# Norm means by rounded matmuls, and four smaller matmul jobs of a decoder trunk recast

## The chip, the cores and the metric

The kernel runs on one core of a Trainium2 chip. The time is device microseconds of that core, the median of several runs. Its engines are named as the profile names them: PE (matmuls; PEld is its weight load), DVE, ACT, POOL and SP. All of a launch's work is in one program; each engine works through its own list of instructions in order and waits on semaphores for the others. Matmul results stand in PSUM, in banks of 128 x 512 numbers.

## The reference

One sequence of 512 tokens with 1024 features passes four steps, each behind a root-mean-square norm: an attention layer (MLA), a squared-ReLU MLP, a gated linear attention (GLA) and a second MLP. A last norm ends it. All is float32.

```python
def rms_norm(x, gain):
    y = x * rsqrt(mean(x * x, axis=-1) + EPS)
    return y * gain

for i in range(2):
    xn = rms_norm(x, norm_mix[i])
    x = x + (mla_mixer(xn, ...) if i == 0 else gla_mixer(xn, ...))
    x = x + square(relu(rms_norm(x, norm_mlp[i]) @ w_up[i])) @ w_down[i]
return rms_norm(x, final_norm)

# MLA: a low-rank latent c_kv is normed too, and gives keys and values
kv = rms_norm(c_kv, kv_norm) @ w_ukv
# GLA, within a chunk of 64 tokens; b is the running sum of the log gates, per feature
attn[t, s] = sum_d q[t, d] * k[s, d] * exp(b[t, d] - b[s, d])     # for s <= t
```

On the diagonal of attn the decay is 1, so attn[t, t] is the sum over d of q k alone.

## The kernel before

Activations lie with features on the 128 partitions and the 512 tokens along the free axis, so x is eight tiles of 128 x 512 (xT). A product is made of three rounded ones: each float32 operand is split into a rounded high part (the type fp32r, an ACT copy) and the low rest (a DVE subtraction), and PE adds high x high, high x low and low x high. That is `mm3` (L120 to L122); the split is `split` (L112 on ACT, L115 on DVE). Where an operand isn't split, PE multiplies in full float32.

`Norm` keeps a running total `acc` of the squares of the eight tiles (ACT squares, DVE adds, L238). `mean` (L255) multiplies `acc` by a constant matrix of 1/1024 in full float32, one product of 512 columns, which sums over the partitions and lays the mean on all of them; `rsqrt` then makes 1/rms. For GLA's input the mean is taken in `finish`, which `a_pair` calls ahead of step k = 5 of the first pair of projections. For each MLP, which runs as a seven-product block scheme on combined operands (`QuadNorm`; T1 to T4 and the x tiles), the place is written out by hand: block steps are popped from two lists, then `combine` of the last row, the mean, some idle products into a scratch bank (`spare`, L1181) and the split of the last combined rows.

In MLA the 1/rms of three norms come as rows (`rows`, 96 x 512: three groups of 32 like rows; L221 ends it). The one for the values is needed on all partitions: a full-precision product of a one-row operand spreads it (L532, bank `wide`), ACT copies it to SBUF (L534), and DVE scales the latent with it (L537). Around it stand the v products and their evacuations (L504 to L508), the rotary tables (L392, with a table load of ACT ahead and one behind), the rotary q products and the key's transposes (L137 of `KS`).

In GLA, 1/rms per token is turned onto the partitions by four one-column products (L1334) and a copy (L1336). Two heads are worked at a time between the projection products. For each head `T` holds gate factors; `grow(m)` scales q and k by them, `same` makes the diagonal of the attention matrix by four 128 x 128 full products (L1454), of which a masked copy (L1455) takes the diagonal, and `small(m)` makes the blocks next to it, for m = 1 up, each by two 128-column full products (L1467) with an ACT copy (L1447) as operand.

The order of the instructions on each engine is set by a scheduler from the order of the code, except where the code says `kept` or `issue_after`. PSUM banks go round by tag: `bank("c")` takes the next bank of that ring.

## Time and profile before

| | before |
|---|---|
| median of 3 runs | 1048.47 us (1047.91 to 1049.2) |
| profiled execution | 1048.56 us, span 1046.5 us, granted clock 0.998 |
| PE / PEld busy | 1037.0 us / 957.7 us |
| DVE / ACT / POOL busy | 858.0 / 645.2 / 92.6 us |

The span runs from the first to the last instruction of the profiled execution, and its time is 2.1 us longer. MLA lasts to about 154 us, its output projection to 188, the first MLP to about 507, GLA with its output projection to 723, the second MLP to about 993. In the chain of waits "x2" counts records, not products: a full-precision product leaves two. The chain dates a matmul from the end of the one before it, about 0.16 us later than the timeline, which dates it from its own start.

### The profile page before, as it was taken

The numbers are of one execution on the slowest core, as the hardware profiler recorded it, in microseconds if no ns is written. First come the engines' busy times: TensorE is split into PE (matmuls) and PEld (weight loads), VectorE is DVE, ScalarE is ACT, GpSimd is POOL, SyncE is SP. The second block draws the span as 40 slices with busy tenths as digits, with TensorE's granted clock in tenths as the row PEclk, the third lists the DMA queues.
The fourth block names the chain that finished last, engine by engine and source line by source line (L and its number), as shares of the span: only waits on it lengthen the run. The fifth ranks groups of instructions, "written<-read, shape, count | busy, mean of one in ns | idle before, by whom it ended". The sixth has DMA issues, their size and how long they took to land.

```text
span 1046.5 us, 17929 instructions
## 1 busy us (share of the span) xinstructions
PE 1037.0 (99%) x7252; PEld 957.7 (92%) x7252; DVE 858.0 (82%) x1236; ACT 645.2 (62%) x969; POOL 92.6 (9%) x118
## 2 busy tenths in 40 slices
PE   8999999999999999999999999999999999999997
PEld 7788888999999999998788888888999999999986
DVE  6789879899899789976576656678999899799855
ACT  5678755666667777654344645656666667776834
POOL 6400000100000000270000000001000000000000
PEclk9999999999999999999999999999999999999999
DMA  6412016866654664351122221239565655653402
GB/s 200 114 50 63 20 41 200 183 181 162 182 136 128 181 147 119 98 187 55 51 81 81 81 79 56 68 101 230 174 145 155 182 134 152 180 133 90 146 37 81
DMA packets 114946, 127.81 MB, mean 122 GB/s; under 512 B 8640, under 2 KB 86736, under 8 KB 114864
## 3 DMA queue, kind: packets, MB, share of 16 engines
q1 hardware_dynamic: 98832, 108.15, 32.6%
q0 software_dynamic: 13792, 16.80, 10.5%
q10 hardware_dynamic: 2240, 1.73, 0.5%
q8 instruction: 57, 0.93, 0.4%
q14 instruction: 25, 0.20, 0.1%
HBM read 124.56 MB, written 2.10 MB: 121 GB/s over the span
## 4 chain that ended last, share of the span: by engine, by line
PE 98%; DMA 1%; DVE 0%; issue 0%; ACT 0%; SPq 0%; DVEq 0%
PE ps L844 51%; PE ps L120 13%; PE ps L122 13%; PE ps L121 13%; PE ps L137 2%; PE ps L1467 1%; DMA wraw_ckv<-in_mla_w_in_dram 1%; PE ps L1502 1%; PE ps L696 0%; PE ps L695 0%; PE ps L692 0%; PE ps L693 0%; PE ps L694 0%; PE ps L1454 0%; PE ps L255 0%; PE ps L1356 0%
## 5 line engine op out<-in xcount | busy, mean ns | idle before, releaser
L112 ACT ACTIVATE wh<-raw 128x1024 fp32r<-128x1024 f32 x208 | 219.4, 1058 | 133.0 <-PE ps L844 74.9
L115 DVE TENSOR_TENSOR wl<-raw,wh 128x1024 fp32r<-128x1024 f32 x208 | 252.0, 1221 | 18.6 <-ACT wh L112 18.2
L844 PE MATMUL ps<-h,wh 128*128 128x256 f32 x1344 | 166.6, 276 | 0.0
L844 PEld LDWEIGHTS ps<-h,wh 128*128 128x128 f32 x1344 | 159.2, 188 | 0.0
L120 PE MATMUL ps<-set,wh 128*128 128x512 f32 x232 | 91.5, 395 | 1.0 <-ACT set L245 1.0
L121 PE MATMUL ps<-set,wh 128*128 128x512 f32 x232 | 91.0, 392 | 0.7 <-DVE set L246 0.6
L122 PE MATMUL ps<-set,wl 128*128 128x512 f32 x232 | 90.6, 391 | 0.0
L844 PE MATMUL ps<-h,wl 128*128 128x256 f32 x672 | 90.1, 276 | 0.0
L897 POOL DMA_DIRECT2D raw<-in_mlp_w_up_dram x20 | 25.8, 1291 | 688.0 <-DVE raw L950 307.3
L844 PEld LDWEIGHTS ps<-h,wl 128*128 128x128 f32 x672 | 82.7, 188 | 0.0
L112 ACT ACTIVATE wh<-wraw 128x1024 fp32r<-128x1024 f32 x41 | 43.1, 1057 | 53.2 <-PE ps L121 25.8
L909 ACT ACTIVATE q<-q 128x512 f32<-128x512 f32 x64 | 40.3, 631 | 51.5 <-DVE q L908 51.5
L115 DVE TENSOR_TENSOR h<-q,h 128x1024 fp32r<-128x1024 f32 x44 | 53.6, 1219 | 9.0 <-ACT h L112 9.0
L120 PE MATMUL ps<-wh,set 128*128 128x512 f32 x144 | 59.5, 413 | 0.0
L121 PE MATMUL ps<-wl,set 128*128 128x512 f32 x144 | 56.3, 391 | 0.0
L122 PE MATMUL ps<-wh,set 128*128 128x512 f32 x144 | 56.2, 391 | 0.0
L115 DVE TENSOR_TENSOR wl<-wraw,wh 128x1024 fp32r<-128x1024 f32 x41 | 50.4, 1229 | 6.8 <-ACT wh L112 6.6
L120 PEld LDWEIGHTS ps<-set,wh 128*128 128x128 f32 x232 | 43.5, 188 | 10.7 <-ACT set L245 1.7
L121 PEld LDWEIGHTS ps<-set,wh 128*128 128x128 f32 x232 | 43.6, 188 | 10.4 <-DVE set L246 1.4
L122 PEld LDWEIGHTS ps<-set,wl 128*128 128x128 f32 x232 | 43.6, 188 | 9.0
L112 ACT ACTIVATE h<-q 128x1024 fp32r<-128x1024 f32 x44 | 46.0, 1048 | 0.9 <-DVE q L1057 0.6
L121 PE MATMUL ps<-hl,wh 128*128 128x512 f32 x96 | 37.4, 389 | 0.0
(522 smaller groups left out, 2780.6 us busy)
## 6 DMA issues: line engine op xcount, KB each, us to landing
raw<-in_mlp_w_down_dram SPq DMA_DIRECT2D x38, 1024.0 KB, 5.2
raw<-in_mlp_w_up_dram SPq DMA_DIRECT2D x70, 512.0 KB, 5.2
wraw<-in_gla_w_in_dram SPq DMA_DIRECT2D x11, 1024.0 KB, 5.3
raw<-in_mlp_w_up_dram POOLq DMA_DIRECT2D x20, 512.0 KB, 7.3
raw<-in_mlp_w_down_dram POOLq DMA_DIRECT2D x6, 1024.0 KB, 9.3
wraw<-in_mla_w_o_dram SPq DMA_DIRECT2D x8, 512.0 KB, 4.9
wraw<-in_gla_w_o_dram SPq DMA_DIRECT2D x8, 512.0 KB, 4.9
wraw_qn<-in_mla_w_uq_dram SPq DMA_DIRECT2D x6, 256.0 KB, 3.4
```

The source lines that it names most:

```text
L112: raised.append(order(ACT.activation(hi, src, AF.Copy)))
L115: return lo_eng.tensor_tensor(lo, src, f(hi), ALU.subtract)
L120: PE.matmul(psum, wh, xh, start=start, stop=False, **kw)
L121: PE.matmul(psum, wh, xl, start=False, stop=False, **kw)
L122: PE.matmul(psum, wl, xh, start=False, stop=stop, **kw)
L137: PE.transpose(psum, src, ident[: src.shape[0], : src.shape[0]])
L844: return PE.matmul(p[:, m * TH : (m + 1) * TH], w[i][:, k - k0, m * P : (m + 1) * P], x[k][j], start=start, stop=stop, skip_group_check=True,)
L897: POOL.dma_start(t, rows(half, trail), accum_op=ALU.add)
L909: ACT.activation(qs, qs, AF.Square)
L1467: PE.matmul(p[:, :, r], side[m][:, sl], joined(o, e), start=True, stop=True)
L1502: PE.matmul(out_, kj, mv, start=True, stop=True)
```

## The change

Six places change.

1. The constant of the means is rounded, and `parted` splits `acc` into a high part (ACT, in the buffer of 1/rms) and a low part (DVE). `mean` is two rounded products. In the MLPs the split stands between the two block steps ahead of the last combined rows, with the second step's, and the last rows', evacuations ordered behind it; the spare products are three instead of four. For GLA's input the mean moves from step 5 to step 6.
2. In MLA four copies within SBUF, issued by ACT, lay the 32 like rows onto all 128 partitions, in place of the product and its copy.
3. In GLA, 1/rms per token comes from a product with the identity and a sum along the row, both on DVE.
4. The diagonal comes from q k on DVE, split, and summed over the partitions by four rounded products of 256 columns with a matrix of ones.
5. The blocks of m = 1 likewise, by two rounded products; their ACT copy goes.
6. One MLP operand buffer always stands at the same offset. The last norm's two products read the constant as full float32.

```diff
@@ -179,12 +179,8 @@
     DVE.memset(causal, 0.0)
     POOL.affine_select(causal, causal, [[-1, P]], ALU.is_ge, NEG, base=0, channel_multiplier=1)
 
-    def inv_tile(n, pool):
-        t = pool.tile([P, P], F32, name=f"inv{n}")
-        DVE.memset(t, 1.0 / n)
-        return t
-
-    inv_d = inv_tile(D, const)
+    inv_d = const.tile([P, P], F32R, name="inv_d")
+    DVE.tensor_scalar(inv_d, ones128, 1.0 / D, None, ALU.mult)
 
 
 
@@ -250,12 +246,18 @@
             self.scaled(j, src)
             self.square(src)
 
-        def mean(self):
+        def parted(self, order=lambda i: i):
+            self.parts = sb.tile([P, S], F32R, tag="rstd", bufs=1, name=uname("acc_hi")), tmp((P, S), F32R)
+            return order(split(self.acc, *self.parts, order=order))
+
+        def mean(self, order=lambda i: i):
             self.ms = bank("c")
-            return PE.matmul(self.ms, self.inv, self.acc, start=True, stop=True)
+            for n, part in enumerate(self.parts):
+                order(PE.matmul(self.ms, self.inv, part, start=n == 0, stop=n == 1))
 
         def finish(self):
             if self.ms is None:
+                self.parted()
                 self.mean()
             m = self.ms
             r = sb.tile([P, S], F32, tag="rstd", bufs=1, name=uname("rstd"))
@@ -406,7 +408,7 @@
 
     def a_pair(psums, w, nrm):
         for k in range(ND):
-            if k == 5:
+            if k == 6:
                 nrm.finish()
             for j in range(2):
                 mm3(psums[j], cut(w[j], slice(None), k), nrm.out[k], k == 0, k == ND - 1)
@@ -489,6 +491,9 @@
         PE.matmul(means, mean_q, q_sq[0], start=False, stop=True)
         rows = sb.tile([3 * RB, S], F32, tag="rstd", bufs=1, name=uname("rstd"))
         rsqrt(rows, means, S, row_eps)
+        r_kv = f(slot("B"))
+        for i in range(P // RB):
+            ACT.dma_start(r_kv[i * RB : (i + 1) * RB], rows[:RB])
 
 
         raw = pool_of("stage").tile([P, 2, MH, VD], F32, tag="wraw", bufs=2, name="wraw_v")
@@ -528,10 +533,6 @@
                 else:
                     evac_v(t, hf, p)
             if t == 1:
-                wide = bank("c")
-                PE.matmul(wide, ones128[0:1], rows[0:1], start=True, stop=True)
-                r_kv = sb.tile([P, S], F32, tag="rstd", bufs=1, name=uname("rstd"))
-                ACT.activation(r_kv, wide, AF.Copy)
                 for j in range(2):
                     y = tmp()
                     DVE.scalar_tensor_tensor(y, pkv[j], gcol("kvn", 2 * layer + j), r_kv, ALU.mult, ALU.mult)
@@ -859,7 +860,7 @@
             for k, m in steps:
                 one(1, 0, k, m, False, end and k == 3)
 
-        Q, wide, turn, fills = {}, {}, [0, None], []
+        Q, wide, turn, fills = {}, {}, [0], []
 
         def up_block(b):
             fh, s = b % 2, b // 2
@@ -1018,9 +1019,7 @@
                 turn[0] ^= 1
                 if turn[0]:
                     h = dp.tile([P, 8 * TH + 40], F32R, tag="h1", name=uname("h"))
-                    c = 0 if turn[1] != s else 40
-                    h = h[:, c : c + 8 * TH].rearrange("p (i k t) -> p i k t", i=2, k=4)
-                    turn[1] = s
+                    h = h[:, 40:].rearrange("p (i k t) -> p i k t", i=2, k=4)
                 else:
                     h = dp.tile([P, 2, 4, TH], F32R, tag="h0", name=uname("h"))
                 split(t, h[:, 0], h[:, 1])
@@ -1188,14 +1187,18 @@
             wide[b] = halves(wide_raw())
         for b, t in enumerate(halves(wide_raw())):
             fills[b](t)
-        for b in range(2):
-            blocks[b].pop(0)()
+        blocks[0].pop(0)()
+        low = nrm.parted(kept)
+        high = raised[-1]
+        with tc.issue_after(high.ins):
+            blocks[1].pop(0)()
         t = nrm.combine(KH - 1, dp.tile([P, 4, TH], F32, tag="q", bufs=6, name=uname("q")))
-        kept(nrm.mean())
-        spare(mp.tile([P, 4 * TH], F32, tag="d", bufs=2, name=uname("ps")), 4)
+        nrm.mean(kept)
+        spare(mp.tile([P, 4 * TH], F32, tag="d", bufs=2, name=uname("ps")), 3)
         made[1]["21"] = piece(made[1]["a12"], KH, 256)
         kept(cut_at[-1])
-        kept(nrm.combined(KH - 1, t))
+        with tc.issue_after(low.ins), tc.issue_after(high.ins):
+            kept(nrm.combined(KH - 1, t))
         pad(up, PADS["up"])
         nrm.finish()
         nrm.total(KH - 1)
@@ -1329,11 +1332,12 @@
         next(rest)
 
 
-        pr = bank("c")
-        for t in range(NT):
-            PE.matmul(pr[:, t : t + 1], nrm.rstd[0:1, t * P : (t + 1) * P], one_t[0:1, 0:1], start=True, stop=True)
+        own_token = tmp((P, NT, P))
+        DVE.tensor_tensor(
+            own_token, nrm.rstd.rearrange("p (t c) -> p t c", t=NT), ident.unsqueeze(1).to_broadcast([P, NT, P]), ALU.mult
+        )
         rtok = sb.tile([P, NT], F32, tag="rtok", name="rtok")
-        DVE.tensor_copy(rtok, pr[:, :NT])
+        DVE.reduce_sum(rtok, own_token, AX.X)
 
 
 
@@ -1407,6 +1411,8 @@
 
 
         A_of = [gp.tile([P, S], F32, tag=f"A{i}", name=f"A{i}") for i in range(2)]
+        ones_r = gp.tile([P, P], F32R, tag="ones_r", name="ones_r")
+        ACT.activation(ones_r, ones128, AF.Copy)
         for A in A_of:
             POOL.memset(A, 0.0)
         AT = {}
@@ -1418,6 +1424,7 @@
             k, qd = both[:, :S], both[:, S:]
             at = AT[h] = {}
             side = {}
+            own, near = [], []
 
             def blocks(t, m, odd):
                 return t.rearrange("p (n b c) -> p n b c", b=2, c=m)[:, :, odd]
@@ -1427,9 +1434,27 @@
 
             def grow(m):
                 if m == 0:
+                    if not own:
+                        both_ = tmp()
+                        DVE.tensor_tensor(both_, q, k, ALU.mult)
+                        own.extend(tmp((P, S), F32R) for _ in range(2))
+                        split(both_, *own)
                     return
                 if m == 1:
                     DVE.tensor_tensor(qd, q, T[1], ALU.mult)
+                    pairs_ = gp.tile([P, 256], F32, tag="E", bufs=3, name=uname("E"))
+                    for a in range(2):
+                        half = slice((1 - a) * 256, (2 - a) * 256)
+                        DVE.tensor_tensor(
+                            pairs_[:, a * P : (a + 1) * P].unsqueeze(2),
+                            blocks(k[:, half], 1, 0),
+                            blocks(qd[:, half], 1, 1),
+                            ALU.mult,
+                        )
+                    t = tmp((P, S), F32R)
+                    near.extend((t[:, :256], t[:, 256:]))
+                    split(pairs_, *near)
+                    return
                 else:
                     g = m // 2
                     d = T[g].rearrange("p (n b) -> p n b", b=2)
@@ -1448,10 +1473,15 @@
 
             def same():
                 p = bank("c")
-                for t in range(NT):
-                    sl = slice(t * P, (t + 1) * P)
-                    c = (t ^ 2) * P
-                    PE.matmul(p[:, c : c + P], k[:, sl], q[:, sl], start=True, stop=True)
+                for r in range(2):
+                    for n, part in enumerate(own):
+                        PE.matmul(
+                            p[:, (1 - r) * 256 : (2 - r) * 256],
+                            ones_r,
+                            part[:, r * 256 : (r + 1) * 256],
+                            start=n == 0,
+                            stop=n == 1,
+                        )
                 DVE.copy_predicated(
                     A.rearrange("p (t c) -> p t c", t=NT),
                     ident_i.unsqueeze(1).to_broadcast([P, NT, P]),
@@ -1460,8 +1490,12 @@
 
             def small(m):
                 n2 = 64 // m
-                p = bank("c")[:, :256].rearrange("p (a r n c) -> p a r n c", a=2, r=2, c=m)
-                for r in range(2):
+                p = bank("c")[:, :256]
+                if m == 1:
+                    for n, part in enumerate(near):
+                        PE.matmul(p, ones_r, part, start=n == 0, stop=n == 1)
+                p = p.rearrange("p (a r n c) -> p a r n c", a=2, r=2, c=m)
+                for r in range(2 if m > 1 else 0):
                     sl = slice(r * P, (r + 1) * P)
                     o, e = blocks(k[:, 256:][:, sl], m, 0), blocks(qd[:, :256][:, sl], m, 1)
                     PE.matmul(p[:, :, r], side[m][:, sl], joined(o, e), start=True, stop=True)
@@ -1718,8 +1752,8 @@
 
         def mean(self):
             self.ms = bank("b")[:, :TH]
-            PE.matmul(self.ms, inv_d, self.acc, start=True, stop=False)
-            PE.matmul(self.ms, inv_d, self.sq, start=False, stop=True)
+            PE.matmul(self.ms, f(inv_d), self.acc, start=True, stop=False)
+            PE.matmul(self.ms, f(inv_d), self.sq, start=False, stop=True)
 
         def finish(self):
             r = sb.tile([P, TH], F32, tag="rstd", bufs=1, name=uname("rstd"))
```

ACT in MLA, from the 1/rms rows to the rotary key (`set` is v or q in SBUF, `KS` the rotary key), before:

```order
L131 ACTIVATE tmp_499<-tmp_497 96x512
L507 ACTIVATE set_538<-ps_517,cols 128x512
...
L507 ACTIVATE set_564<-ps_557,cols 128x512
L534 ACTIVATE rstd_570<-ps_568 128x512
L507 ACTIVATE set_591<-ps_584,cols 128x512
...
L507 ACTIVATE set_602<-ps_595,cols 128x512
L504 ACTIVATE set_613<-ps_606,cols 128x512
...
L504 ACTIVATE set_622<-ps_615,cols 128x512
L392 ACT_TABLE_LOAD
L392 ACTIVATE rope_tabs<-rope_turns 128x256
L127 ACT_TABLE_LOAD
L570 ACTIVATE set_661<-ps_651 128x512
```

and in the change:

```order
L131 ACTIVATE tmp_499<-tmp_497 96x512
L496 DMA set_506<-rstd_496 32x512 x4
L512 ACTIVATE set_543<-ps_522,cols 128x512
...
L512 ACTIVATE set_603<-ps_596,cols 128x512
L571 ACTIVATE set_662<-ps_652 128x512
L509 ACTIVATE set_614<-ps_607,cols 128x512
L509 ACTIVATE set_623<-ps_616,cols 128x512
L394 ACT_TABLE_LOAD
L394 ACTIVATE rope_tabs<-rope_turns 128x256
L127 ACT_TABLE_LOAD
```

The product's copy is replaced by four issues right behind the rows. The first rotary q evacuation (before L570, now L571) now stands ahead of the last two of v and of the table loads.

PE there, from the last rotary q products on, before:

```order
L121 MATMUL ps_687<-set_644,cq2h 128x512
L122 MATMUL ps_687<-set_643,cq2l 128x512
L120 MATMUL ps_725<-cq0h,wh_721 128x512
L121 MATMUL ps_725<-cq0l,wh_721 128x512
...
L122 MATMUL ps_741<-ckv1h,wl_718 128x512
L137 MATMUL ps_756<-ident,KS 128x128 x4
L137 MATMUL ps_762<-ident,KS 128x128 x4
L120 MATMUL ps_768<-cq0h,wh_721 128x512
```

and in the change:

```order
L121 MATMUL ps_688<-set_645,cq2h 128x512
L122 MATMUL ps_688<-set_644,cq2l 128x512
L137 MATMUL ps_757<-ident,KS 128x128 x4
L120 MATMUL ps_726<-cq0h,wh_722 128x512
L121 MATMUL ps_726<-cq0l,wh_722 128x512
L120 MATMUL ps_742<-ckv0h,wh_718 128x512
...
L122 MATMUL ps_742<-ckv0h,wl_719 128x512
...
L137 MATMUL ps_763<-ident,KS 128x128 x4
```

Four of the eight transposes of the rotary key now stand ahead of the first q product (`cq0h`).

DVE in the second MLP, around the last combined rows (`q`), before:

```order
L238 TENSOR_TENSOR acc_7549<-acc_7549,tmp_7840 128x512
L298 SCALAR_TENSOR_TENSOR q_7932<-xT,gains,q_7932 128x256
L305 TENSOR_TENSOR xT<-xT 128x256
L299 SCALAR_TENSOR_TENSOR q_7932<-xT,gains_less,q_7932 128x256
L300 SCALAR_TENSOR_TENSOR q_7932<-xT,gains_less,q_7932 128x256
L301 SCALAR_TENSOR_TENSOR q_7932<-xT,gains_less,q_7932 128x256
L115 TENSOR_TENSOR wl_7946<-raw_7771,wh_7945 128x1024
L115 TENSOR_TENSOR T3l_7950<-q_7932,T3h_7949 128x1024
```

and in the change:

```order
L234 TENSOR_TENSOR acc_7598<-acc_7598,tmp_7889 128x512
L300 SCALAR_TENSOR_TENSOR q_7985<-xT,gains,q_7985 128x256
L307 TENSOR_TENSOR xT<-xT 128x256
L301 SCALAR_TENSOR_TENSOR q_7985<-xT,gains_less,q_7985 128x256
L302 SCALAR_TENSOR_TENSOR q_7985<-xT,gains_less,q_7985 128x256
L303 SCALAR_TENSOR_TENSOR q_7985<-xT,gains_less,q_7985 128x256
L115 TENSOR_TENSOR mt_7953<-acc_7598,acc_hi_7952 128x512
L115 TENSOR_TENSOR wl_7999<-raw_7820,wh_7998 128x1024
L115 TENSOR_TENSOR T3l_8003<-q_7985,T3h_8002 128x1024
```

The low half of the totals (`mt`) is subtracted behind the four steps of the combined rows and ahead of a weight's low part.

PE in GLA at the diagonal of the first pair of heads (`ps_6128` and `ps_6149` are the sums, the products of 512 columns are projections), before:

```order
L121 MATMUL ps_6097<-wl_6101,set_5711 128x512
L122 MATMUL ps_6097<-wh_6100,set_5712 128x512
L1454 MATMUL ps_6128<-q_5940,qk_5982 128x128 x4
L120 MATMUL ps_6094<-wh_6134,set_5736 128x512
L121 MATMUL ps_6094<-wl_6135,set_5736 128x512
```

and in the change:

```order
L121 MATMUL ps_6105<-wl_6156,set_5741 128x512
L1478 MATMUL ps_6149<-tmp_6127,ones_r 128x256
L122 MATMUL ps_6105<-wh_6155,set_5742 128x512
L120 MATMUL ps_6106<-wh_6155,set_5741 128x512
L121 MATMUL ps_6106<-wl_6156,set_5741 128x512
L1478 MATMUL ps_6149<-tmp_6128,ones_r 128x256
L1478 MATMUL ps_6149<-tmp_6127,ones_r 128x256
L1478 MATMUL ps_6149<-tmp_6128,ones_r 128x256
L122 MATMUL ps_6106<-wh_6155,set_5742 128x512
```

The four rounded products (`ones_r`) stand among the projections, the first two on the two halves of the split apart.

## The prediction

> **What bounds the kernel now.** I read four views, in this order: the busy shares of the page, the waits of PE, the chain that ended last around each place of the change, and the timelines of DVE and ACT there. First the shares.
>
> ```profile
> PE 1037.0 (99%) x7252; PEld 957.7 (92%) x7252; DVE 858.0 (82%) x1236; ACT 645.2 (62%) x969; POOL 92.6 (9%) x118
> ```
>
> A share of 99% does not say that PE is the limit, since pipelined matmuls look long. The waits of PE do:
>
> ```profile
> PE ps L1640 <- DVE ones L175: 1.2, 1, 1.2
> PE ps L120 <- ACT set L245: 1.0, 2, 0.8
> PE ps L121 <- DVE set L246: 0.6, 1, 0.6
> ```
>
> These three, 2.8 us together, are all of them, and their lines belong to the start (ones, the first norm). Behind it PE waits for nothing in a span of 1046.5 us. So a matmul that is taken away shows in full, unless what it gave cover to comes late; and a new wait of PE shows in full too. The prices of PE's work are the spacings in the chain:
>
> ```profile
> 504.05 0.23 PE ps L121
> 507.22 0.86 PE ps L255 x2
> 517.64 0.98 PE ps L1334 x8
> 518.62 0.40 PE ps L1356
> 519.02 0.23 PE ps L1357
> 534.07 0.89 PE ps L1454 x8
> 544.99 0.46 PE ps L1467 x4
> 193.88 0.86 PE ps L255 x2
> 194.73 0.47 PE ps L1181 x4
> 48.90 1.05 PE ps L532 x2
> 49.95 0.43 PE ps L120
> ```
>
> A rounded product of 512 columns takes 0.23 us (L121; L1356 and L120 just behind a full-precision one take 0.40 and 0.43). One of 256 columns takes 0.47 / 4 = 0.12 (L1181). A full-precision one of 512 columns, two records, takes 0.86. So a full-precision product costs nearly four rounded ones, and two rounded ones (hi and lo) in its place save about half.
>
> The Trainium skill, "Perfetto Trace Analysis", Identifying the Most-Contended Engine, calls matmul busy time a bad measure and asks for the weight loads' share instead. Here that share is 92%, which taken by itself would leave 8% of head-room and let savings vanish; the list of three waits and the back-to-back rows disagree, so the sum goes by these.
>
> **The change, part by part.** Each is costed on PE first, then for what the new work of DVE and ACT makes late.
>
> GLA's input norm (before's L255 at 507.22): 0.86 becomes 2 x 0.23, so -0.40. The split of the totals (ACT, then DVE, 0.6 and 0.7 us) has the step from k = 5 to k = 6 of the pair loop to hide in, six products or 1.4 us; nothing added.
>
> 1/rms per token: four transposing products (L1334) go, and DVE multiplies by the identity and reduces instead. 0.98 goes, and the product behind them falls from 0.40 to 0.23: -1.15. DVE's two operations are about 0.7 us each and are needed only by the v evacuations, tens of products later: nothing added.
>
> The diagonal: 0.89 (L1454) becomes four products of 256 columns, 0.47: -0.42 for each of 4 heads, -1.68. The neighbours' blocks (m = 1): 0.46 (L1467) becomes two, 0.23: -0.23 a head, -0.92. Together GLA gives -0.40 - 1.15 - 1.68 - 0.92 = -4.15.
>
> Against this stand the new inputs. These rows are of the first pair of heads:
>
> ```profile
> 528.86 0.68 DVE L1322 TENSOR_TENSOR qk<-ps,rstd 128x512 f32<-128x512 f32 x1
> 533.36 2.08 ACT L131 ACTIVATE T<-T 128x1020 f32<-128x1020 f32 x2 [2.12 <-DVE T L1402]
> 534.45 0.69 DVE L1432 TENSOR_TENSOR qk<-q,T 128x512 f32<-128x512 f32 x1
> ```
>
> Before, the diagonal needed only k, there from 529.54 and used at 534.07, 4.5 us later. Now it needs q*k (0.69), a rounding on ACT (0.6) and a subtraction on DVE (0.7): 2.0 us a head, 4.0 for two if nothing overlaps. That fits under 4.5 just so. ACT was idle 2.1 us ahead of its row at 533.36. The two subtractions and two products stand among the gate's short DVE steps, so the gates T come later, by up to 2.8 us for a pair; the m = 1 blocks had 544.99 - 535.14 = 9.9 us to spare. Lower bound 0, upper bound one uncovered chain of 2.0 for each of two pairs, 4.0; I take 0.3, near the bottom, because the cover is longer than the chain.
>
> First MLP. The mean saves 0.40 at 193.88, the spare products go from four to three, 0.12: -0.52. But there is a new wait. Without the old 1/rms product the ring of PSUM banks turns by one, so the seed product, at the start of this MLP, now writes the bank of the last output product, and must wait until its residual add has read it.
>
> ```profile
> 187.87 0.40 PE L1181 MATMUL ps<-x0h 128*128 128x256 f32 x2
> 188.07 0.69 DVE L820 TENSOR_TENSOR xT<-ps,xT 128x512 f32<-128x512 f32 x1 [0.68 <-PE ps L122]
> ```
>
> The add ends at 188.76, so PE stands still from 187.87 until then, with a little for the signal: +0.94. Lower bound 0, if the bank isn't the same; nothing behind it costs more, since PE's later inputs move with it. The Trainium skill, "Perfetto Trace Analysis", Optimizing Tensor Performance, says that independent groups should rotate through PSUM banks so that one's evacuation overlaps the next; before's rows fit that, and this place would break it. If the waiting were nothing, as before's list of waits has it everywhere, the forecast would be 1044.1. Net here +0.42.
>
> Second MLP: again -0.52, and here the banks don't clash, but the low half of the totals is late.
>
> ```profile
> 724.90 0.61 ACT L237 ACTIVATE tmp<-xT 128x512 f32<-128x512 f32 x1
> 725.70 0.69 DVE L238 TENSOR_TENSOR acc<-acc,tmp 128x512 f32<-128x512 f32 x1
> 726.84 0.58 ACT L944 ACTIVATE ps<-ps 128x512 f32<-128x512 f32 x1
> 728.62 0.48 DVE L301 SCALAR_TENSOR_TENSOR q<-xT,gains_less,q 128x256 f32<-128x256 f32 x1
> 729.15 1.02 PE L255 MATMUL ps<-acc,inv 128*128 128x512 f32 x2
> ```
>
> The totals end at 726.39. ACT rounds them behind L944, about 727.4 to 728.0, so DVE could subtract from 728.0; but in the order the subtraction stands behind the last of the combined rows' steps, which ends at 729.10. It runs to 729.79. The high product starts at 729.15 and ends 0.23 later, and the low one waits from 729.38 to 729.75: +0.37. The lower bound is 0, the upper one 0.7, the whole subtraction. Net -0.15. In the first MLP the same chain lies under the 0.94.
>
> MLA: the product that spread the 1/rms row (L532) goes: 1.05 and the 0.20 by which 49.95 is too long, -1.25. Four copies of 64 KB on ACT's queue take its place.
>
> ```profile
> 45.66 0.69 DVE L221 SCALAR_TENSOR_TENSOR rstd<-tmp,tmp 96x512 f32<-96x512 f32 x1
> 50.63 1.40 DVE L537 SCALAR_TENSOR_TENSOR tmp<-ps,gains,rstd 128x512 f32<-128x512 f32 x2
> L1349 ACTq DMA_DIRECT2D tmp<-in_gla_w_gk_up_dram x6: 322/434/597, 509.3 to 513.1; - x6
> DMA to landing us min/median/max: 1.7/1.8/2.2
> ```
>
> The trace has no copy inside SBUF. The nearest rows are ACT's small loads L1349: 0.43 to issue, 1.8 to land. Rows end at 46.35; four issues take 1.7; the last lands at 46.35 + 1.7 + 1.8 = 49.9. The reader (L537) starts at 50.63 at the earliest, and about 2 us later in the new order: cover of 0.7 to 2.2 us. ACT issues while it had nothing to do (its next row waits until 47.27), so it is late by 0.8 at most.
>
> But the 1.25 is given back. The chain that makes the rotary key is:
>
> ```profile
> 57.75 0.40 PE L122 MATMUL ps<-set,cq2l 128*128 128x512 f32 x1
> 55.94 0.67 ACT L504 ACTIVATE set<-ps,cols 128x512 f32<-128x512 f32 x1
> 56.62 1.28 ACT L392 ACT_TABLE_LOAD   x1
> 57.92 0.42 ACT L392 ACTIVATE rope_tabs<-rope_turns 128x256 f32<-128x256 f32 x1
> 58.35 1.28 ACT L127 ACT_TABLE_LOAD   x1
> 60.72 0.41 ACT L112 ACTIVATE KS<-tmp 128x256 fp32r<-128x256 f32 x1
> 61.16 0.42 DVE L115 TENSOR_TENSOR KS<-tmp,KS 128x256 fp32r<-128x256 f32 x1
> 61.02 0.84 ACT L112 ACTIVATE wh<-wraw_qn 128x768 fp32r<-128x768 f32 x1
> 64.10 0.39 PE L120 MATMUL ps<-cq0h,wh 128*128 128x512 f32 x1
> 67.51 1.03 PE L137 MATMUL ps<-ident,KS 128*128 128x128 f32 x8
> ```
>
> In the new order the first q evacuation stands ahead of the last two v evacuations and of the table load. It waits for a product that ended at 58.15 and now ends at 56.90. Then 0.6 for it, 2 x 0.67, 1.3 for the load and 0.42: the tables end at 60.6 instead of 58.34, 2.2 us later. All that follows moves by that: KS is whole at 61.58 + 2.2 = 63.8, the rounded weights at 61.86 + 2.2 and an evacuation (0.6) = 64.6. In the new order four of the eight KS transposes stand ahead of the first q product; PE is there at 64.10 - 1.25 = 62.85 and waits until 63.8, transposes (0.4), and starts the product at 64.6, 0.5 after before, with 0.4 of the transposes already done. So +0.1 in place of -1.25; bounds -1.25 (the chain is in time) and +0.5 (the early transposes take nothing from later).
>
> The sum: -4.15 + 0.3 (GLA) + 0.42 (first MLP) - 0.15 (second) + 0.1 (MLA) = -3.5. From the profiled execution's 1048.56 that is 1045.1; it stands 0.09 over the median of the runs, so the forecast for a median is 1045.0. The last norm's product changes its name only.
>
> **The rivals.** A, everything saved shows: no bank wait, no late low half, a rotary chain in time. Then -4.15 - 0.52 - 0.52 - 1.25 = -6.4, 1042.1. For it: PE never waited before, and the order was laid out anew. Against it: the rows of 188.07 and 728.62.
>
> B, GLA's gain is lost to the splits: each pair of heads waits for its q*k chain, 2 x 2.0 us instead of 0.3, which takes 3.7 back: 1048.7, no change. For it: the chain of 4.0 fills a cover of 4.5. Against it: DVE and ACT both stood idle ahead of their rows there.
>
> C, slower: the copied rows land late. DVE's in-order queue holds L537, and behind it the v subtractions and the key's chain, so PE comes to stand. The time decides from cover: beyond 2.2 us of lateness every further one is lost. The cover ends near 52.1 in the new order. To be slower than before at all they must land after 52.1 + 3.5 = 55.6, and for over 0.2% after 57.7; a landing 10 us behind the last issue (48.05) gives 1045.0 + 5.9 = 1050.9. Against it: L1349's 1.7 to 2.2.
>
> D, the products don't get cheaper: rounded products with the same weights twice cost as much as what they replace (a limit of weight loads, 92% busy). Then only the tokens' and the spare products go, -1.15 - 0.24, and 0.1 + 0.3 + 0.94 + 0.37 come in: +0.3, 1048.8, no change. Against it: 0.23 beside 0.86 for the same shape, each load hidden. The Trainium skill's rule on the weight loads' share, named above, would make this the likelier one.
>
> **How the numbers follow.** The forecast has 0.52, A 0.20, B 0.16, C 0.06, D 0.06. A measurement of this kernel tells a change from none at about 0.2%, 2.1 us: faster is under 1046.4. Forecast and A lie there, 0.72; B and D, 0.22, within; C 0.06, slower. The forecast's own range is 1043.7 to 1046.3, from the bounds of the waits (a missing bank wait -0.9, a lost MLA wait -1.2; 1.3 more in GLA). To hold 8 of 10 the range goes down past A to 1041.8 and up part of the way to B, 1047.8.
>
> **What would show it.** In the profile after: no wait of PE in GLA over 0.5 us; a wait of PE for the residual add at 187 us of about 0.9; one for the low half near 725 of about 0.4; PE idle for KS near 63 for about 0.9; 1/rms copies landing within 4 us of the rows' end; the diagonal's four products in 0.47. The prediction is wrong if PE stalls in GLA for longer than the 0.42 it saves a head, if the copies land after 52, or if the mean's two products take more than 0.46.

## The result: slower, by a rhythm of PE in the second MLP

| | before | after |
|---|---|---|
| median | 1048.42 us (1047.91 to 1049.2, 4 runs) | 1054.3 us (1054.1 to 1054.95, 4 runs) |
| profiled span | 1046.5 us | 1053.1 us |

The ratio of after to before is 1.0054, 95% interval 1.0039 to 1.0069. The forecast was 1045.0 us, faster. First the page's busy shares and the list of all waits of PE, of the changed kernel (columns: engine and line, what it waited for, us in total, times, longest):

```profile
PE 1041.6 (99%) x7216; PEld 961.9 (91%) x7216; DVE 866.6 (82%) x1260; ACT 648.5 (62%) x976; POOL 93.4 (9%) x118
```

```profile
PE ps L137 <- DVE KS L115: 1.3, 1, 1.3
PE ps L1674 <- DVE ones L175: 1.2, 1, 1.2
PE ps L1180 <- DVE xT L821: 0.8, 1, 0.8
PE ps L120 <- ACT set L241: 0.5, 1, 0.5
PE ps L121 <- DVE set L242: 0.3, 1, 0.3
PE ps L256 <- DVE mt L115: 0.2, 1, 0.2
```

The three waits that were forecast stand there (L137 for the rotary key, L1180 for the residual add, L256 for the low half), 2.3 us together, and none in GLA. They can't explain a loss of 5.9 us beside savings. To find it, follow one instruction through both traces (timeline starts):

| where | before | after | difference |
|---|---|---|---|
| first q product of MLA (cq0h) | 64.10 | 64.19 | +0.09 |
| seed product, first MLP | 187.87 | 188.74 | +0.87 |
| first product behind that MLP's mean | 195.05 | 195.60 | +0.55 |
| first product of the second MLP | 723.30 | 719.92 | -3.38 |
| first product behind its mean | 730.48 | 727.07 | -3.41 |
| first product of its last two blocks (hh) | 992.15 | 998.43 | +6.27 |
| end | 1046.51 | 1053.11 | +6.61 |

Up to 727 us the total is the prediction's: -3.41, where the sum had -3.5 (its terms are not, as is shown below). Then 9.7 us are lost between 730 and 992 us of before, where the change has no instruction besides the operand's offset. The busy time of each engine in two stretches shows how. Columns: the stretch, its sum, then busy time and count of PE, PEld, DVE, ACT and POOL, the granted clock, DMA share and GB/s. Before:

```profile
200.00:300.00 100.00, 100.00 (x883) 100.00 (x883) 92.97 (x90) 65.66 (x77) 5.11 (x4) 1.00 0.60 163
800.00:900.00 100.00, 100.00 (x883) 100.00 (x882) 88.15 (x80) 67.95 (x78) 3.85 (x3) 1.00 0.57 161
```

After:

```profile
200.00:300.00 100.00, 100.00 (x885) 100.00 (x884) 93.31 (x91) 64.97 (x77) 5.11 (x4) 1.00 0.58 163
800.00:900.00 100.00, 100.00 (x852) 100.00 (x851) 83.88 (x77) 65.02 (x74) 3.85 (x3) 1.00 0.54 154
```

In the first MLP PE does 885 records in 100 us, in the second 852. PE is busy without a gap in both, at a granted clock of 1.00, and waits for nothing: each product of 256 columns takes 117.8 ns from one start to the next instead of 113.3 (means over 740 to 980 us and 240 to 455 us of the changed kernel). Over the 2,300 products of this stretch that is 10 us. The slower spacing stands for all operands alike and repeats exactly, every third weight load reading 192 ns instead of 188. These are the rows around the mean:

```profile
725.53 0.40 PE L845 MATMUL ps<-x3h,w 128*128 128x256 f32 x2
725.77 0.40 PE L256 MATMUL ps<-acc_hi,inv_d 128*128 128x512 f32 x1
726.37 0.50 PE L256 MATMUL ps<-mt,inv_d 128*128 128x512 f32 x1 [0.21 <-DVE mt L115]
726.72 0.51 PE L1180 MATMUL ps<-x0h 128*128 128x256 f32 x3
727.07 0.28 PE L845 MATMUL ps<-x4h,wh 128*128 128x256 f32 x1
727.18 0.28 PE L845 MATMUL ps<-x4l,wh 128*128 128x256 f32 x1
```

PE stalls for the low half of the totals at 726 us, and from 726.8 on every product takes 117 to 120 ns, until the first 512-column products at 998. I call this the slow rhythm and the other the fast one. The same place before:

```profile
728.67 0.40 PE L844 MATMUL ps<-x2h,w 128*128 128x256 f32 x2
728.91 0.40 PE L844 MATMUL ps<-x3h,w 128*128 128x256 f32 x2
729.15 1.02 PE L255 MATMUL ps<-acc,inv 128*128 128x512 f32 x2
729.60 1.04 PE L1181 MATMUL ps<-x0h 128*128 128x256 f32 x4
730.95 0.28 PE L844 MATMUL ps<-x5h,wh 128*128 128x256 f32 x1
731.06 0.28 PE L844 MATMUL ps<-x5l,wh 128*128 128x256 f32 x1
```

The 24 products just ahead of the mean (operand `w`) stand 0.12 us apart in both kernels, each weight load reading 192 ns. So the stall isn't what makes PE slower than 113.3 ns at first. The kernels differ in what follows: before is at 113.3 ns from 730.8 us on, after stays slow. In the first MLP the changed kernel too comes back to the fast rhythm behind its mean.

The Trainium skill ("Perfetto Trace Analysis", Identifying the Most-Contended Engine) would judge PE by MFU and the weight loads' share rather than by matmul busy time. Here that share is 100% in both rhythms, as matmul busy time is, so neither share tells them apart. The count of records in a stretch does, and MFU, as work over time, goes with it.

### The profile page after: what moved, and what is told of

Read it like the earlier page. It is cut to its first block, busy times and chain, and to the rows that moved or that the text cites. A ratio compares the mean times of both kernels' runs of the same rounds, so it can differ in the third digit from the quotient of the medians.

```text
span 1053.1 us, 17901 instructions
## 1 busy us (share of the span) xinstructions
PE 1041.6 (99%) x7216; PEld 961.9 (91%) x7216; DVE 866.6 (82%) x1260; ACT 648.5 (62%) x976; POOL 93.4 (9%) x118
## 4 chain that ended last, share of the span: by engine, by line
PE 94%; ACT 2%; DVE 1%; DMA 1%; issue 1%; ACTq 0%; SPq 0%; DVEq 0%
PE ps L845 51%; PE ps L120 12%; PE ps L122 12%; PE ps L121 12%; PE ps L137 2%; PE ps L1501 1%; DMA xT<-in_x_dram 1%; PE ps L1536 1%; PE ps L697 0%; PE ps L696 0%; PE ps L693 0%; PE ps L695 0%; PE ps L694 0%; DMA wraw_kn<-in_mla_w_ukv_dram 0%; ACT wh L112 0%
## 5 line engine op out<-in xcount | busy, mean ns | idle before, releaser
L845 PE MATMUL ps<-h,wh 128*128 128x256 f32 x1344 | 169.0, 278 | 0.0
L845 PEld LDWEIGHTS ps<-h,wh 128*128 128x128 f32 x1344 | 161.6, 189 | 0.0
L122 PE MATMUL ps<-hh,wl 128*128 128x512 f32 x96 | 37.4, 389 | 0.0
```

What stands on the lines that cost most here:

```text
L122: PE.matmul(psum, wl, xh, start=False, stop=stop, **kw)
L845: return PE.matmul(p[:, m * TH : (m + 1) * TH], w[i][:, k - k0, m * P : (m + 1) * P], x[k][j], start=start, stop=stop, skip_group_check=True,)
```

## The experiments

The first four undo one suspect each: the late low half, the three spare products, the operand's offset, the split mean. In the table at the end stand the records of PE from 880 to 980 us: 883 or so is the fast rhythm, 851 the slow one.

**e1: the low half in time.**

```diff
-        t = nrm.combine(KH - 1, dp.tile([P, 4, TH], F32, tag="q", bufs=6, name=uname("q")))
+        with tc.issue_after(low.ins), tc.issue_after(high.ins):
+            t = nrm.combine(KH - 1, dp.tile([P, 4, TH], F32, tag="q", bufs=6, name=uname("q")))
```

> The changed kernel, with the rounding of the totals on ACT and the subtraction of their low half on DVE ordered ahead of the steps of the last combined rows, in both MLPs. Its second MLP spaces its 256-column products at 117.8 ns throughout, where the kernel before has 113.3. Theory W (wait): PE's short wait of 0.2 us between the two mean products leaves PE in a slower rhythm that lasts until the shape changes; without the wait the second MLP goes back to 113.3 ns and the time to about 1054.3 - 9.9 = 1044.4. Theory S (three spare products instead of four) and theory H (the MLP operand at one offset): the rhythm stays at 117.8 and the time within 0.5 of 1054.3. A mean computed in two rounded products as such (theory M): also no change.

Measured: 1054.2, 1055.1, 1065.0 and 1065.6 us. In the profiled execution the mean runs without a wait and is followed by the fast rhythm (727.5 us), but the slow one begins at 746.8 us and stays. So the wait is not the only way into it. The edit also makes a weight's low part late, and PE stands still for it at 737 us:

```profile
737.80 0.51 PE L845 MATMUL ps<-T0h,wl 128*128 128x256 f32 x2 [0.22 <-DVE wl L115]
```

The products at 737.8 and 738.0 come 0.38 and 0.11 us late, and a few products on PE is in the fast rhythm again: a stall need not lead to the slow one. Two of the runs are 10 us longer still; that is what the slow rhythm in both MLPs would cost, though no profile shows one of these.

**e2: four spare products.**

```diff
-        spare(mp.tile([P, 4 * TH], F32, tag="d", bufs=2, name=uname("ps")), 3)
+        spare(mp.tile([P, 4 * TH], F32, tag="d", bufs=2, name=uname("ps")), 4)
```

> The changed kernel with four spare products behind the mean, as before, instead of three. Theory S: the fourth one restores the rhythm; second MLP at 113.3 ns, about 1044.7. Theories W, H and M: no change of the rhythm, 1054.3 + 2 x 0.12 = 1054.5.

Measured: 1055.23 us (1054.48 to 1055.56). The wait for the low half is there, and the slow rhythm from it on.

**e3: the operand at alternating offsets.**

```diff
-                    h = h[:, 40:].rearrange("p (i k t) -> p i k t", i=2, k=4)
+                    c = 0 if turn[1] != s else 40
+                    h = h[:, c : c + 8 * TH].rearrange("p (i k t) -> p i k t", i=2, k=4)
+                    turn[1] = s
```

> The changed kernel with the MLP operand at alternating offsets again, as before. Theory H: second MLP at 113.3 ns, about 1045. Theories W, S and M: still 117.8 ns there, and the short slower stretches of the kernel before return in the first MLP (3 stretches of about 5 us at 116.7): 1054.3 + 0.5 = 1054.8.

Measured: 1047.83 us (1045.14 to 1049.59, 10 runs), ratio 0.9988 (0.9975 to 1.0001). Theory H came nearer to the time, but the trace, which is of the slowest of the ten runs (1049.59 us), shows another thing than either theory had. The stretches of 780 to 840 and 880 to 980 us (columns: stretch, sum, PE busy and count, granted clock, DMA share, GB/s):

```profile
780.00:840.00 60.00, 60.00 (x512) 1.00 0.56 163
880.00:980.00 100.00, 100.00 (x883) 1.00 0.50 140
```

The slow rhythm is there too (512 records in 60 us; the kernel before has 532), from 749.5 us on, behind a product that comes 0.04 us late, and it ends at 862.7, at the end of a stretch in which the operand stands at offset 0. In such a stretch products take 116.7 ns, in the kernel before as well (236 to 242 us, 320 to 326 and so on, six in all), and what follows it runs fast. The first such stretch of this MLP, about 769 to 775 us, did not end the slow rhythm. So the alternating offset, which looked like a small cost, can end the slow rhythm: it did at one of its turns here.

**e4: the MLP means in full precision.**

```diff
-        low = nrm.parted(kept)
...
-        nrm.mean(kept)
+        kept(PE.matmul(nrm.ms, f(nrm.inv), nrm.acc, start=True, stop=True))
```

> The changed kernel with the mean of both MLPs by one full-precision product of the unsplit totals again (no split, no late low half), with three spare products, everything else changed. Theory M and theory W: second MLP at 113.3 ns; 1054.3 - 9.7 + 2 x 0.4 - 0.4 = 1045.0. Theories S and H: still 117.8 ns, about 1054.7.

Measured: 1055.3 us (1053.86 to 1057.0). Theories W and M both miss. The rhythm is fast behind the mean, and turns slow at 751.9 us, behind one product that comes 0.1 us late:

```profile
751.43 0.39 PE L845 MATMUL ps<-T3h,wl 128*128 128x256 f32 x2
751.66 0.37 PE L845 MATMUL ps<-x4h,wh 128*128 128x256 f32 x1
751.87 0.28 PE L845 MATMUL ps<-x4l,wh 128*128 128x256 f32 x1
```

It writes a bank that ACT's copy (751.01, 0.58 us long) has just read, so 0.07 us were left; in the kernel before the same product follows the copy by 0.18 us and isn't late. The next one should come 0.11 us after 751.66 and comes 0.21 after. This gave the next theory: if any break starts the slow rhythm, 0.12 us of idle work should prevent it. (In this kernel's first MLP a product comes 0.04 us late at 437 us, and the fast rhythm is back after six products.)

**e5: e4 with the fourth spare product.**

```diff
-        spare(mp.tile([P, 4 * TH], F32, tag="d", bufs=2, name=uname("ps")), 3)
+        spare(mp.tile([P, 4 * TH], F32, tag="d", bufs=2, name=uname("ps")), 4)
```

> The changed kernel with the MLP means in full precision again (as in e4_mlp_full_mean) and, unlike there, four spare products instead of three. In e4 the slow rhythm of 117.8 ns began at a stall of 0.1 us at 751.7 us, where PE waited for ACT's copy of a finished sum with 0.07 us between the copy's end and the product; the kernel before has 0.18 us at this place and no stall. Theory W2 (any short stall of PE in an MLP starts the slow rhythm, and with the operand at one offset nothing ends it): 0.12 us more of spare work takes the stall away, the second MLP runs at 113.3 ns to its end, and the time is 1054.3 - 9.7 + 0.6 = 1045.2, 9 us below e4. Theory H2 (the operand at one offset is slow of itself in the second MLP): 117.8 ns again and 1055.

Measured: 1045.78 us (1044.49 to 1047.85, 10 runs), ratio 0.9982 (0.9973 to 0.9992). One more idle product, 0.12 us of work in each MLP, makes the kernel 9.5 us faster than e4. The same place has no gap now:

```profile
749.38 0.39 PE L845 MATMUL ps<-T3h,wl 128*128 128x256 f32 x2
749.61 0.28 PE L845 MATMUL ps<-x4h,wh 128*128 128x256 f32 x1
749.72 0.28 PE L845 MATMUL ps<-x4l,wh 128*128 128x256 f32 x1
```

Theory H2 falls with it: the operand at one offset isn't slow of itself.

**e6: the kernel before with the operand at one offset.**

```diff
-                    c = 0 if turn[1] != s else 40
-                    h = h[:, c : c + 8 * TH].rearrange("p (i k t) -> p i k t", i=2, k=4)
-                    turn[1] = s
+                    h = h[:, 40 : 40 + 8 * TH].rearrange("p (i k t) -> p i k t", i=2, k=4)
```

> The kernel before with the MLP operand at one offset, and nothing else changed. Theory W2: it has no stall in its MLPs, so no slow rhythm begins; its six stretches of about 6 us at 116.7 ns (the operand at offset 0) go, 6 x 0.17 = 1.0 us: 1047.4. Theory H2: the second MLP runs at 117.8 ns throughout, 1048.4 + 9.7 = 1058.

Measured: nine of ten runs at 1046.28 to 1048.30 us, one at 1056.6; median 1047.18, ratio 1.0001 (0.9982 to 1.002). In the profile the six slower stretches are gone and the second MLP is fast throughout. The usual gain is the forecast 1 us, and the single run shows the price: about 9 us more, the size of one MLP in the slow rhythm (this run has no profile).

**e7: the kernel before with three spare products.**

```diff
-        spare(mp.tile([P, 4 * TH], F32, tag="d", bufs=2, name=uname("ps")), 4)
+        spare(mp.tile([P, 4 * TH], F32, tag="d", bufs=2, name=uname("ps")), 3)
```

> The kernel before with three spare products instead of four in each MLP. Theory W2: PE comes 0.12 us earlier to the product that waits for ACT's copy at 752 us, where 0.18 us were left, so it stalls there; the slow rhythm begins and lasts to the end of one of the next stretches with the operand at offset 0 (777 or 862 us): 25 x 0.039 = 1.0 or 110 x 0.039 = 4.3 us more, 1049.2 to 1052.5. Theory H2 and the plain account (a product less, 2 x 0.12): 1048.2.

Measured: median 1047.98 us, eight runs at 1046.95 to 1048.52 and two at 1051.5 and 1051.75. In the profiled one the slow rhythm begins at 747.9 us, without a stall there, and ends at 751.3 in the middle of like products, so it cost only 0.13 us. The two long runs are of the size of the upper case (1052.5), but without a profile. Median and interval (1.0005, 0.9993 to 1.0016) say no change.

**e8: fourteen spare products ahead of the second MLP's mean, none behind.** The helper's column index goes round by four, so that fourteen fit the bank.

```diff
+        idle = mp.tile([P, 4 * TH], F32, tag="d", bufs=2, name=uname("ps"))
+        if final:
+            spare(idle, 14)
         nrm.mean(kept)
-        spare(mp.tile([P, 4 * TH], F32, tag="d", bufs=2, name=uname("ps")), 3)
+        if not final:
+            spare(idle, 3)
```

> The changed kernel with fourteen spare products ahead of the second MLP's mean and none behind it: they cover the low half's wait and let PE come later to the product at 749 us. Theory W2: no stall, 113.3 ns to the end: at the mean's end it is 2.6 us ahead of the kernel before instead of 3.4, and stays there: about 1045.6 with what the operand's one offset saves in the second MLP. Theory H2: 117.8 ns, about 1055.

Measured: 1055.56 us (1055.25 to 1057.27): theory W2 fell. The fourteen spare products stand 0.12 us apart, like the products ahead of them. No product waits, yet the slow rhythm stands from the mean on:

```profile
727.76 0.39 PE L256 MATMUL ps<-mt,inv_d 128*128 128x512 f32 x1
728.00 0.28 PE L845 MATMUL ps<-x4h,wh 128*128 128x256 f32 x1
728.11 0.28 PE L845 MATMUL ps<-x4l,wh 128*128 128x256 f32 x1
728.23 0.28 PE L845 MATMUL ps<-x4h,wh 128*128 128x256 f32 x1
```

A stall is thus one kind of break; a change of shape (two products of 512 columns) is another. What follows the break seems to decide, which e9 tests by one line.

**e9: e8 with three spare products behind the mean.**

```diff
-        if not final:
-            spare(idle, 3)
+        spare(idle, 3)
```

> As e8 (the changed kernel, fourteen spare products ahead of the second MLP's mean, which cover the wait for the low half), with three spare products behind the mean as well, as the changed kernel has. In e8 no product waited, and yet the rhythm of 117.8 ns stood from the first 256-column product behind the mean. Theory R (the rhythm is drawn anew at each break of the stream of like products, by a stall or by other shapes, and what stands right behind the break decides: here the spare products, which have one operand for both inputs): with three behind an unbroken mean the second MLP starts as the first one does in the changed kernel, at 113.3 ns: about 1046.0. Theory P (two rounded mean products lead to the slow rhythm in the second MLP, whatever stands around them): 117.8 ns to the end, 1056.

Measured: 1046.41 us (1045.19 to 1049.22, 10 runs), ratio 0.9989 (0.998 to 0.9998). Theory P falls, and R holds for this pair: 0.35 us of idle products behind the mean, and the kernel is 9.2 us faster than e8 (the kernel before, run beside each, gave 1047.51 here and 1048.11 there, so 0.6 of it isn't the edit's). Its stretch from 880 to 980 us has 885 records. Here the MLP means are in two rounded products, as the change has them, so these alone are not at fault. Nor do spare products alone decide: with the wait for the low half left in, e2's four were followed by the slow rhythm. The last 23 us of e9's first MLP (433.6 to 456.6 us) are slow too.

**e10 to e12: the other steps, without the rhythm.** All start from e5. e10 takes the banks of the spare products ahead of the seed's (first diff), e11 puts MLA back (second diff), and e12 adds to e11 the alternating offset of e3.

```diff
+        idle = mp.tile([P, 4 * TH], F32, tag="d", bufs=2, name=uname("ps"))
         spare(mp.tile([P, 512], F32, tag="seed", name=uname("ps")), 2)
...
-        spare(mp.tile([P, 4 * TH], F32, tag="d", bufs=2, name=uname("ps")), 4)
+        spare(idle, 4)
```

```diff
-        r_kv = f(slot("B"))
-        for i in range(P // RB):
-            ACT.dma_start(r_kv[i * RB : (i + 1) * RB], rows[:RB])
...
+                wide = bank("c")
+                PE.matmul(wide, ones128[0:1], rows[0:1], start=True, stop=True)
+                r_kv = sb.tile([P, S], F32, tag="rstd", bufs=1, name=uname("rstd"))
+                ACT.activation(r_kv, wide, AF.Copy)
```

> e5 (the changed kernel with the MLP means in full precision and four spare products), with the PSUM banks of the MLPs laid out so that the seed product doesn't write the bank of the last output product. The prediction's step on the bank: the wait of 0.8 to 0.9 us for the residual add ahead of each clashing MLP goes, 1045.78 - 0.9 = 1044.9. If the wait covers something that is late anyway, no change: 1045.8.

Measured: 1043.98 us (1043.48 to 1047.89, 7 runs), ratio 0.9966 (0.9954 to 0.9977). The wait for the residual add is gone from the list; the gain over e5 is 1.8 us by the medians, of which 0.9 was forecast; 0.6 of it is again the difference between the kernel before beside each. From the first q product to the seed product e5 takes 0.76 us more than the kernel before and e10 0.24 less, so 1.0 us is the bank's; the rest is no more than e5's spread.

> e5 with MLA as it was before (the 1/rms row spread by a product and an ACT copy, no copies by DMA), which also turns the ring of banks back. The prediction's steps: the copies' saving of 1.25 is given back by the rotary chain (+0.1 net), and the bank's wait is 0.9, so both go: 1045.78 - 0.1 - 0.9 = 1044.8. If the copies do save their 1.25: 1045.78 + 1.25 - 0.9 = 1046.1.

Measured: 1043.16 us (1042.47 to 1044.12, 5 runs), ratio 0.9953 (0.9941 to 0.9966), the fastest kernel here. It is 0.8 us faster than e10, which has the copies in MLA and no bank clash either: the copies don't save their 1.25 us and if anything cost a little (the two intervals overlap, so this is no more than "not faster").

> e11 with the MLP operand at alternating offsets, as before. Theory R: six stretches at 116.7 ns come back (+1.0 us) and end every slow rhythm that begins, so the runs lie closer together: 1045.8 with no run above 1050; e11's fastest runs are a microsecond faster, and single ones may be up to 10 us slower.

Measured: 1043.95 us, all five runs within 1043.75 to 1044.21, ratio 0.9961 (0.9947 to 0.9974). As forecast it is 0.8 us slower than e11 and steadier. In e11's profile the last 23 us of the second MLP are in the slow rhythm (from 964.3 us), in e12's nothing behind the mean is. All of e10 to e12 came 0.9 to 1.9 us below their forecasts, which started from e5; 0.6 of that is the difference just named.

| run | median us | records of PE, 880 to 980 us | slow rhythm in the second MLP, behind its mean |
|---|---|---|---|
| before | 1048.42 | 883 | none |
| after | 1054.3 | 851 | 727 to 998 |
| e1 | 1060.02 | 852 | from 747 |
| e2 | 1055.23 | 851 | from 727 |
| e3 | 1047.83 | 883 | 750 to 863 |
| e4 | 1055.3 | 851 | from 752 |
| e5 | 1045.78 | 884 | none |
| e6 | 1047.18 | 885 | none |
| e7 | 1047.98 | 883 | 748 to 751 |
| e8 | 1055.56 | 851 | from 728 |
| e9 | 1046.41 | 885 | none |
| e10 | 1043.98 | 884 | none |
| e11 | 1043.16 | 879 | from 964 |
| e12 | 1043.95 | 884 | none |

## Why the prediction was wrong

The step that failed is "Net -0.15" for the second MLP, and behind it the sentence that a new wait of PE shows in full, and so at its own length. The wait for the low half was as long as forecast (0.6 us from the high product to the low one, 0.38 more than a product takes, against 0.37). But behind it PE didn't come back to the fast rhythm, and what followed ran at 117.8 ns for 270 us. That is 9.7 us, a cost that no wait, busy share or clock in the profile names. The wait isn't shown to be the one cause: e8 went slow without it, and e3 came back fast behind it. Two terms were missing. The operand's offset (the sixth edit) was costed at nothing and not even weighed; it gave 0.55 us in the first MLP (885 records against 883) and took away the stretches of which one ended the slow rhythm in e3. The spare products were costed as 0.12 us of idle work; e8 and e9 show that they can set what follows the mean.

The profile of before had the clue: the products ahead of the mean stand 0.12 us apart, the four spare ones, which I quoted, take 0.47 us, and the 2,304 behind them take 261.68 us, 0.1136 each. I took the first for the price of any product of 256 columns.

That -3.41 at 727 us is so near to -3.5 is partly luck. The five terms are -0.08 in MLA (forecast +0.1), +0.63 for the first MLP's bank and mean (+0.42), -0.55 for the operand's offset (nothing), -3.38 in GLA (-3.85) and -0.03 up to the second mean's end (-0.15). Without the term that I didn't have, the forecast ones come to -2.86.

The other steps, each against the trace of after:

- **GLA**, forecast -3.85: from the last product ahead of step k = 5, at 506.83 us in both, to the second MLP it takes 213.1 us instead of 216.5, -3.38. The chain's rows of the mean and of three of the diagonal's four products:

```profile
508.58 0.45 PE ps L256 x2
...
535.17 0.36 PE ps L1478 x3
```

  Two mean products take 0.45, as forecast; these three of the diagonal 0.12 each. No wait in GLA: rival B didn't come, and the 0.3 taken for it wasn't needed. Against -4.15 there is 0.8 us missing, in part by the prices: counted from each one's start to the next product's, the sixteen products of the diagonal take 2.19 us and the eight of the neighbours' blocks 1.11, where 1.88 and 0.92 were forecast. That is 0.5; what the rest is stays open.
- **The bank**, forecast +0.94: the seed product comes 1.18 us behind the last output product instead of 0.23, +0.95, and e10 shows the wait gone with the bank. (The +0.87 in the table has MLA's -0.08 in it; the 0.78 below is the idle time only.) The mean and the spare product then save 0.32 instead of 0.52; the products between the stall and those with `w` run at 117.8 ns there.

```profile
187.56 0.39 PE L122 MATMUL ps<-set,wl 128*128 128x512 f32 x1
188.74 0.50 PE L1180 MATMUL ps<-x0h 128*128 128x256 f32 x2 [0.78 <-DVE xT L821]
```

- **MLA**, forecast +0.1: +0.09 at the first q product, where four of the key's transposes are already done, and -0.08 at the last output product (187.56 against 187.64), with the wait for the key in its place (forecast 0.9, measured 1.26).

```profile
L496 ACTq DMA_DIRECT2D set<-rstd x4: 597/606/612, 45.6 to 47.5; - x4
DMA to landing us min/median/max: 2.0/2.0/2.1
63.44 0.66 PE L137 MATMUL ps<-ident,KS 128*128 128x128 f32 x4 [1.26 <-DVE KS L115]
```

  The copies take 0.6 to issue and 2.0 to land (0.43 and 1.8 were taken), so the last, issued at 47.5, lands at 49.5, ahead of its reader at 52.1: rival C didn't come either. (Landing counts from the start of an issue, so the prediction's 49.9 has the last issue in it twice.) One link was missed: the issues hold ACT until 48.1, and in the new order ACT's rounding of the last rotary weights stands behind them and behind the first v evacuation; so the buffer comes free later, and the next weights are fetched at 50.23 instead of 43.03. Before, then after (SyncE's queue):

```profile
43.03 0.92 SPq L582 DMA_DIRECT2D wraw_kn<-in_mla_w_ukv_dram  x2
```

```profile
50.23 1.76 SPq L583 DMA_DIRECT2D wraw_kn<-in_mla_w_ukv_dram  x2
```

  ACT then waits 1.19 us for them, until 54.7, in the middle of the chain to the key. How much of the 1.26 comes from this is not shown.
- **The low half**, forecast +0.37: +0.38. The prediction's own ends, 729.38 and 729.79, would have given 0.41.
- **Rival D** fell: the products that were recast got cheaper, as the rows above show. None of the rivals is what happened.

## What stays open

Which rhythm a break leads to is not settled. After one and the same wait of 0.38 us for the low half the changed kernel and e2 went slow, and e3 went fast until 749 us. Products that come late by 0.04 to 0.11 us are followed by the slow rhythm in e3 (749 us), e4 (752) and e11 (964), but by the fast one in e4's first MLP (437) and in e10 (965), and in e1 (737) so is one that comes 0.38 us late. e10 and e11 are the nearest pair: the same product of the second MLP waits for DVE's low part of a weight, 0.09 us late in e10 and 0.11 in e11. Behind it stand, in e10 and then in e11 (columns as in e3):

```profile
966.00:986.00 20.00, 20.00 (x179) 1.00 0.48 160
```

```profile
965.00:985.00 20.00, 20.00 (x172) 1.00 0.46 152
```

In e1 (746.9 us), e7 (747.9) and e9 (433.6) the slow rhythm begins with no product more than about 0.01 us late. Shown are: the rhythm's size; that once it stood it lasted in most runs until products of another shape came, in e3 until the end of a stretch with the operand at offset 0, and in e7 for 3.4 us only; that one spare product more (e4 to e5) and three behind the mean (e8 to e9) change which one follows. Which single part of the change made its second MLP slow is not shown: e1 takes the wait away and e2 puts the fourth spare product back, each alone, and both stay slow; e3, e5 and e9 become fast, wholly or for the most part, by three different edits. Why 113.3 and 117.8 ns, and why every third weight load, nothing here tells.

## What to carry to other kernels

Where one engine is full, count its instructions per stretch of time in both traces before believing any sum of savings: a change of 4% in the spacing of like instructions is worth more than every wait on the list. Odd-looking idle products, pads and offsets in a tuned kernel may hold such a spacing; cost an edit that touches them by what the stream does afterwards, not by their own length. Savings that bring the full engine closer to its inputs need slack at the next tight hand-over (here 0.18 us at 752 us), or they may be paid for there, as in e4.

## What was unexpected in the hardware

- Products of 256 columns in fp32r run at 113.3 ns or, with the same operands and a granted clock of 1.00, at 117.8 ns, for up to 270 us on end; a third value, 116.7 ns, belongs to one operand's offset in SBUF, and a fourth, 120 ns, stands in both kernels for the 24 products ahead of each MLP's mean.
- A product 0.1 us late can be followed by the slower spacing for the rest of an MLP (e4, e11) or by six products of recovery (e10), and 0.12 to 0.35 us of idle products kept PE out of it in e5 and e9.
- A copy of 64 KB within SBUF takes 0.61 us to issue on ACT's queue and lands 2.0 us behind the start of its issue.
